# Gate and up columns of a SwiGLU block as one block, with three of its eight k pairs by Strassen's seven products

## The chip, the cores and the metric

The kernel runs on one core of one Trainium2 chip. The metric is the device time of one execution in microseconds (us). The time before is the median of three runs, 1590.43 us (1590.37 to 1591.91).

The engines are named as in the profile: PE (TensorE, matrix products), PEld (its weight loads), DVE (VectorE), ACT (ScalarE), POOL (GpSimd), SP (SyncE, which issues the weight loads from memory here).

## The reference

One layer of a streaming encoder on 256 tokens of width 2048: a norm, an input projection, three token mixers (a recurrence, chunked attention, a state space), gates, an output projection with a residual, and then the part that the change is in:

```python
h = rmsnorm(x, norm_ffn_g[l])
x = x + (jax.nn.silu(h @ w_ffn_gate[l]) * (h @ w_ffn_up[l])) @ w_ffn_down[l]
...
return rmsnorm(x, norm_final_g)
```

`w_ffn_gate` and `w_ffn_up` are 2048 x 5632, `w_ffn_down` is 5632 x 2048, all float32.

## The kernel before

**Precision by three products.** Every weight tile is split into a high part (`hi`, rounded to the type fp32r by an ACT copy) and a low part (`lo`, the exact difference `raw - hi`, a DVE subtraction). Activations are split the same way (`h2h`, `h2l` for the normed input of the feed-forward part). A product is then three matmuls: high x high, low x high, high x low (lines 277 to 279).

**Units and steps.** All weights stream through one list of steps (`steps`, filled by `add_job`, line 225). A step is two k tiles of 128 rows by 512 columns; its body (line 266) issues 2 k tiles x 2 halves of the tokens x 3 = 12 matmuls of 128x512. A job is one block of 512 output columns; its two accumulators (`mm`, one per half of the tokens) lie in two of eight PSUM banks. In PSUM four banks are for `mm`, two for small results (`sm`), and two for the `bu` tile of the state space.

**What sets the order.** The order is written out by hand. The loop at line 1146 does, at step d: issue the load of unit d+5 on SP (four `raw` buffers), copy the high part of unit d+2 on ACT (three `hi` and three `lo` buffers), run what was put off to this step (`later`), issue the matmuls of step d, run what was put off behind them (`later_pe`), and subtract the low part of unit d+2 on DVE. Each engine works through its instructions in that order.

**The feed-forward part.** `ffn_up` (line 998) makes one block n of 512 hidden columns: eight steps of `w_gate`, then eight steps of `w_up`. When the gate sums are done, ACT takes the silu out of PSUM (`sg`); when the up sums are done, DVE multiplies (line 1017); one step later PE turns the product by eight transposes (`at_ps`), and ACT and DVE split it into `at`. Blocks 0 to 5 are part 0 and blocks 6 to 10 part 1; after each part come the columns of `w_down` over the rows of that part. `load_gain` (line 994) loads the gain of the last norm during block 0.

**The rows of `h2`.** In the output projection just before, `turn` (line 976) transposes the residual sum and `parts` (line 980) scales it by the norm's gain and splits it.

Of the kernel before, what the change touches and what calls it, by code (L numbers as in the profile page):

```python
# [27 lines left out]
UK = 2  # L28
RAWB = 4
LEAD = 5  # L30
PARTB = 3
AHEAD = 2
WARM = 9
NORM_STEP = 13
ROOM = 0.4
LO_WEIGHT = 1.22
ROOM_ACT = 1.5
# [23 lines left out]
R_G1, R_G2, R_CW, R_CB, R_BA, R_BX, R_LAM, R_D, R_S5 = 0, 16, 32, 64, 72, 80, 88, 96, 104  # L61
# [58 lines left out]
def trunk(  # L120
# [4 lines left out]
    nc = tc.nc  # L125
# [86 lines left out]
    steps = []  # L212
    raws, his, los = {}, {}, {}
    on_load, on_step, place = {}, {}, {}
    late, late_pe = {}, {}

    def later(n, fn):
# [3 lines left out]
    def later_pe(n, fn):  # L221

        late_pe.setdefault(state["done"] + n, []).append(fn)

    def add_job(src, kt, c0, body, pre=None):

        for k0 in range(0, kt, UK):
            steps.append((src, k0, c0, body, kt, pre if k0 == 0 else None))

    def load_unit(i):  # L230
        if i >= len(steps):
            return
        if i in on_load:
            on_load[i]()
        src, k0, c0 = steps[i][:3]
        raw = wp.tile([P, UK, 512], F32, tag="raw", name="raw", bufs=RAWB)
        raws[i] = raw
        if i > 1:
            nc.sync.dma_start(
                raw, src[k0 * P:(k0 + UK) * P, c0:c0 + 512].rearrange("(k p) n -> p k n", p=P))  # L240
        else:
            for kk in range(UK):
                if i == 0:
                    nc.sync.dma_start(xf[:, kk, :], x_fm[:, kk, :])
                nc.sync.dma_start(raw[:, kk, :], src[(k0 + kk) * P:(k0 + kk + 1) * P, c0:c0 + 512])

    def hi_part(i, kk=slice(None)):
        if i >= len(steps):
            return
        if i not in his:  # L250
            if i in place:
                his[i], los[i] = place[i]()
            else:
                his[i] = wp.tile([P, UK, 512], F32R, tag="hi", name="hi", bufs=PARTB)
                los[i] = wp.tile([P, UK, 512], F32R, tag="lo", name="lo", bufs=PARTB)
        act.copy(his[i][:, kk, :], raws[i][:, kk, :])

    def lo_part(i, kk=slice(None)):
        if i < len(steps):
# [680 lines left out]
    fx = {}  # L940
# [3 lines left out]
    def after_mix():  # L944
# [7 lines left out]
            act.dma_start(fx["x2"], x.rearrange("(h p) d -> p h d", p=P))  # L952
        later_pe(2, residual)

    for n in range(4):
        cs = slice(n * 512, (n + 1) * 512)

        def evac_out(acc, n=n, cs=cs):
            def add():
                x2 = fx["x2"]  # L960
                for h in range(2):
                    vec.scalar_tensor_tensor(x2[:, h, cs], acc[h], 0.5, x2[:, h, cs], ALU.mult, ALU.add)
                later(1, square)
                later_pe(1, turn)

            def square():
                sq = tp.tile([P, 2, 512], F32, tag="t", name="sq")
                for h in range(2):
                    act.activation(sq[:, h, :], fx["x2"][:, h, cs], AF.Square, accum_out=ss4[:, h, n:n + 1])
                if n == 3:  # L970
                    def norm():
                        vec.tensor_reduce(ss, ss4, AX.X, ALU.add)
                        rstd_of(rstd2, ss, scr)
                    later(1, norm)

            def turn():
                for k0 in (4 * n, 4 * n + 2):
                    t = transpose_tokens(lambda h, k: fx["x2"][:, h, k * P:(k + 1) * P], k0, "h2_ps")

# [18 lines left out]
    def ffn_up(part, n, n0):  # L998
        sg = {}

        def evac_gate(acc):
            def do():
                t = fx["fp"].tile([P, 2, 512], F32, tag="sg", name="sg", bufs=2)
                for h in range(2):
                    act.activation(t[:, h, :], acc[h], AF.Silu, scale=rstd2[:, h:h + 1])
                sg[0] = t
            later(1, do)

        def evac_up(acc):
            kb = 4 * (n - n0)  # L1010

            def do():
                if n == n0:
                    at[part] = tuple(fx["fp"].tile([P, 24, S], F32R, tag=f"at{i}", name=f"at{i}") for i in range(2))
                t = sg[0]
                for h in range(2):
                    vec.scalar_tensor_tensor(t[:, h, :], acc[h], rstd2[:, h:h + 1], t[:, h, :], ALU.mult, ALU.mult)
                later_pe(1, turn)

            def turn():  # L1020
                for k0 in (0, 2):
# [5 lines left out]
        add_job(w_gate, KT, n * 512, as_body(lambda: fx["h2"], evac_gate),  # L1027
                (lambda: later_pe(2, load_gain)) if n == 0 else None)
        add_job(w_up, KT, n * 512, as_body(lambda: fx["h2"], evac_up))

    for part, (n0, n1) in enumerate(parts):
        for n in range(n0, n1):
            ffn_up(part, n, n0)
        for c in range(4):
            cs = slice(c * 512, (c + 1) * 512)
            src, kt = w_down[n0 * 512:n1 * 512], 4 * (n1 - n0)
            if part == 1 and c == 3:
                break

            def evac_down(acc, part=part, c=c, cs=cs):  # L1040
                def add():
                    x2 = fx["x2"]
                    for h in range(2):
                        vec.tensor_add(x2[:, h, cs], x2[:, h, cs], acc[h])
                    if part == 1:
                        later(1, square)

                def square():
                    x2 = fx["x2"]
                    sq = tp.tile([P, 2, 512], F32, tag="t", name="sq")  # L1050
                    for h in range(2):
                        act.activation(sq[:, h, :], x2[:, h, cs], AF.Square, accum_out=sq3[:, h, c:c + 1])
                    later(1, scale)

                def scale():
# [175 lines left out]
```

## Time and profile before

| what | value |
|---|---|
| median of three runs | 1590.43 us |
| the profiled execution | 1589.98 us |
| its span, first to last instruction | 1588.2 us |
| PE busy | 1573.7 us (99%), 7193 matmuls and transposes |
| DVE busy | 1028.7 us (65%) |
| ACT busy | 825.1 us (52%) |
| granted clock of PE, mean | 0.998 |

The span is the time between the first and the last instruction of the profiled execution; the rest of its 1589.98 us lies around it. A busy share is a mean over the whole span; the stages differ.

### The profile page before, as it was taken

How to read it: one execution, taken by the hardware profiler on the slowest of the kernel's cores; microseconds unless marked ns; L12 is line 12 of the kernel's file. 1: busy time of each engine (PE TensorE's matmuls, PEld its weight loads, DVE VectorE, ACT ScalarE, POOL GpSimd, SP SyncE). 2: the span in 40 equal slices, each digit the busy share in tenths (PEclk: the TensorE clock that was granted, in tenths of full speed). 3: DMA queues.
4: the chain of work that ended last, by engine and by line, in shares of the span. 5: the costliest groups of instructions: out<-in, count | busy, mean ns of one | idle time of the engine just before them, and what ended most of it. 6: DMA issues, size and time to landing. Idle time of an engine off the chain costs nothing.

```text
span 1588.2 us, 19207 instructions
## 1 busy us (share of the span) xinstructions
PE 1573.7 (99%) x7193; PEld 1296.7 (82%) x7193; DVE 1028.7 (65%) x1183; ACT 825.1 (52%) x1057; POOL 39.8 (3%) x88
## 2 busy tenths in 40 slices
PE   9999999999999999999999999999999999999997
PEld 6888888888888888888888888888888888888885
DVE  5876789988799988566655555454544455545554
ACT  6668675557677645544455444444433444444443
POOL 0011000000000000000000000000000000000000
PEclk9999999999999999999999999999999999999999
DMA  9687757777587766655656665665555666565563
GB/s 326 227 238 222 248 179 211 202 208 192 155 227 196 203 207 186 199 185 187 235 187 212 188 193 184 197 192 186 188 197 192 193 188 192 186 196 190 186 193 127
DMA packets 168558, 317.73 MB, mean 200 GB/s; under 512 B 10625, under 2 KB 23441, under 8 KB 167569
## 3 DMA queue, kind: packets, MB, share of 16 engines
q1 hardware_dynamic: 153632, 296.04, 59.1%
q0 software_dynamic: 11264, 10.49, 3.8%
q10 hardware_dynamic: 3568, 9.98, 1.7%
q8 instruction: 56, 0.92, 0.2%
q14 instruction: 38, 0.30, 0.1%
HBM read 310.17 MB, written 6.30 MB: 199 GB/s over the span
## 4 chain that ended last, share of the span: by engine, by line
PE 97%; DVE 1%; DMA 1%; ACT 0%; issue 0%; SPq 0%; ACTq 0%; DVEq 0%
PE mm L76 93%; PE at_ps L76 1%; PE y_ps L76 1%; PE fm_ps L76 0%; PE bu L76 0%; DVE lo L76 0%; DMA raw<-in_w_in 0%; PE lru_ps L76 0%; PE o_ps L76 0%; PE sc_ps L76 0%; DMA raw<-in_w_ffn_down 0%; DVE res L76 0%; PE h_ps L76 0%; PE mt_ps L76 0%; PE pt_ps L76 0%
## 5 line engine op out<-in xcount | busy, mean ns | idle before, releaser
L76 ACT CAST hi<-raw 128x1024 fp32r<-128x1024 f32 (+1 forms) x546 | 572.5, 1049 | 721.3 <-PE mm L76 677.5
L76 DVE TENSOR_TENSOR lo<-raw,hi 128x1024 fp32r<-128x1024 f32 (+1 forms) x546 | 663.2, 1218 | 432.4 <-ACT hi L76 430.4
L76 PE MATMUL mm<-hi,xth 128*128 128x512 f32 x768 | 303.4, 395 | 1.5 <-ACT hi L76 1.5
L76 PE MATMUL mm<-lo,xth 128*128 128x512 f32 x768 | 299.9, 390 | 0.6 <-DVE lo L76 0.5
L76 PE MATMUL mm<-hi,xtl 128*128 128x512 f32 x768 | 299.2, 390 | 0.0
L76 PE MATMUL mm<-hi,h2h 128*128 128x512 f32 x704 | 274.8, 390 | 0.0
L76 PE MATMUL mm<-lo,h2h 128*128 128x512 f32 x704 | 274.1, 389 | 0.6 <-DVE lo L76 0.6
L76 PE MATMUL mm<-hi,h2l 128*128 128x512 f32 x704 | 273.9, 389 | 0.0
L76 PE MATMUL mm<-hi,at 128*128 128x512 f32 x640 | 197.4, 390 | 0.6 <-ACT hi L76 0.6
L76 PEld LDWEIGHTS mm<-hi,xth 128*128 128x128 f32 x768 | 144.2, 188 | 34.2 <-ACT hi L76 4.6
L76 PEld LDWEIGHTS mm<-lo,xth 128*128 128x128 f32 x768 | 144.2, 188 | 33.2 <-DVE lo L76 2.9
L76 PEld LDWEIGHTS mm<-hi,xtl 128*128 128x128 f32 x768 | 144.3, 188 | 28.6
L76 PEld LDWEIGHTS mm<-lo,h2h 128*128 128x128 f32 x704 | 132.2, 188 | 28.5 <-DVE lo L76 1.1
L76 PEld LDWEIGHTS mm<-hi,h2l 128*128 128x128 f32 x704 | 132.2, 188 | 27.0
L76 PEld LDWEIGHTS mm<-hi,h2h 128*128 128x128 f32 x704 | 132.2, 188 | 27.0
L76 PEld LDWEIGHTS mm<-hi,at 128*128 128x128 f32 x640 | 119.9, 188 | 25.8 <-ACT hi L76 1.1
L76 PE MATMUL mm<-lo,at 128*128 128x512 f32 x320 | 124.6, 389 | 0.5 <-DVE lo L76 0.5
L76 PE MATMUL mm<-hi,yc 128*128 128x512 f32 x256 | 79.1, 390 | 0.0
L76 PEld LDWEIGHTS mm<-lo,at 128*128 128x128 f32 x320 | 60.1, 188 | 13.4 <-DVE lo L76 1.0
L76 PEld LDWEIGHTS mm<-hi,yc 128*128 128x128 f32 x256 | 47.8, 188 | 9.8
L76 PE MATMUL mm<-hi,mth 128*128 128x512 f32 x128 | 50.2, 392 | 0.0
L76 PE MATMUL mm<-lo,mth 128*128 128x512 f32 x128 | 49.8, 389 | 0.0
(181 smaller groups left out, 1297.2 us busy)
## 6 DMA issues: line engine op xcount, KB each, us to landing
raw<-in_w_in SPq DMA_DIRECT2D x190, 512.0 KB, 4.3
raw<-in_w_ffn_gate SPq DMA_DIRECT2D x88, 512.0 KB, 3.5
raw<-in_w_ffn_up SPq DMA_DIRECT2D x88, 512.0 KB, 4.2
raw<-in_w_ffn_down SPq DMA_DIRECT2D x88, 512.0 KB, 4.8
raw<-in_w_branch SPq DMA_DIRECT2D x48, 512.0 KB, 4.7
raw<-in_w_out SPq DMA_DIRECT2D x32, 512.0 KB, 4.6
raw<-in_ssm_w_glu SPq DMA_DIRECT2D x16, 512.0 KB, 4.7
bc<-s_b POOLq DMA_DIRECT2D x24, 128.0 KB, 5.3
```

The costliest lines, as they stand in the source:

```text
L76: return fn(*args, **kw)
```

## The change

Blocks 1 to 10 are made by `ffn_block` in place of `ffn_up`. Block 0 stays as it was.

Gate and up columns of a block run together, with their four sums (two halves of the tokens for gate, two for up) in the four `mm` banks. The sixteen k tiles are eight pairs. Of a pair, the activations form a 2 x 2 matrix of blocks (halves of the tokens by k tiles) and the weights one too (k tiles by gate and up). Three of the eight pairs (`NQ = 3`) are multiplied by the scheme with seven block products instead of eight. It needs sums of the blocks of both matrices:

- of the activations (`left_sums`), made once and split into high and low parts (`lsum`), in the columns n = 0 and n = 1 of the output projection;
- of the weights (`Pair`), made for each pair in each block: `mix` subtracts (1024 wide), `low` makes two more differences (512 wide each) and the low parts; the high parts are ACT copies (`high`). The sums lie in `mix` tiles, their parts in `pmix`.

A pair takes two steps, 9 matmuls in the first and 12 in the second. Three of its products are needed in two or more sums; these lie in the `sm` banks (`p5`, `p1`) and in the `bu` banks (`p67`), and `sum1`, `sum2` and `sum3` add them on DVE after the pairs. `silu` and `product` then add what lies in the `mm` banks. The order of the sixteen steps of a block is `FFN_ORDER`: p0, p1, p2 are the pairs, g and u are steps of gate and up as before. The rows of a pair are loaded by four transfers of 256 KB in place of two of 512 KB, into a tile `praw` with room for two pairs. The transposes of a block's product move into the next block, four of them behind each of two steps. `load_gain` moves to the first columns of `w_down` of part 1.

```diff
+NQ = 3
+FFN_ORDER = 'p0 p0 g p1 p1 u p2 p2 u g g g g u u u'
...
+        if i in paired:
+            return
...
-        act.copy(his[i][:, kk, :], raws[i][:, kk, :])
+        if i in paired:
+            paired[i].high(i)
+        else:
+            act.copy(his[i][:, kk, :], raws[i][:, kk, :])
...
+        if i in paired:
+            paired[i].low(i)
+        elif i < len(steps):
...
+    def left_sums(k0, t):
...
+        if k0 == 0:
+            fx["sum"] = big.tile([P, NQ, 2, 4, P], F32R, tag="B", name="lsum")
+            fx["acc"] = fx["fp"].tile([P, 2, 512], F32, name="acc")
+        w = tp.tile([P, 2, 512], F32, tag="t", name="lw")
+        a = w[:, 0, :].rearrange("p (k s) -> p k s", k=2)
+        sf = w[:, 1, :].rearrange("p (i s) -> p i s", i=4)
+        for i in range(2):
+            act.activation(a[:, i], t[:, i * S:(i + 1) * S], AF.Identity, scale=prm[:, R_G2 + k0 + i:R_G2 + k0 + i + 1])
+        a11, a21, a12, a22 = a[:, 0, :P], a[:, 0, P:], a[:, 1, :P], a[:, 1, P:]
+
+        def sums():
+            act.copy(h2h[:, k0:k0 + 2, :], a)
+            vec.tensor_add(sf[:, 0], a21, a22)
+            vec.tensor_sub(sf[:, 1], sf[:, 0], a11)
+            vec.tensor_sub(sf[:, 2], a11, a21)
+            vec.tensor_sub(sf[:, 3], a12, sf[:, 1])
+
+            def low():
+                act.copy(fx["sum"][:, k0 // 2, 0], sf)
+                vec.tensor_sub(h2l[:, k0:k0 + 2, :], a, h2h[:, k0:k0 + 2, :].bitcast(F32))
+                vec.tensor_sub(fx["sum"][:, k0 // 2, 1], sf, fx["sum"][:, k0 // 2, 0].bitcast(F32))
+            later(1, low)
+        later(1, sums)
+
...
+                        if k0 < 2 * NQ:
+                            left_sums(k0, t)
+                            return
...
+                fx["turn"] = turn
+
+            def turn(k0s=(0, 2)):
+                for k0 in k0s:
...
+    class Pair:
...
+            two = i - self.first
+            for j, src in enumerate((w_gate, w_up) if two == 0 else (w_up, w_gate)):
+                k = 2 * self.q + two
+                nc.sync.dma_start(self.raw[:, 2 * two + j, :], src[k * P:(k + 1) * P, self.n * 512:(self.n + 1) * 512])
+
+        def mix(self, i):
+            if i == self.first:
+                self.t = [tp.tile([P, 2, 512], F32, tag="t", name="mix")]
+                vec.tensor_sub(self.t[0], self.raw[:, 1:3], self.raw[:, 0:2])
+
+        def high(self, i):
+            mixed, raw = fx["mixed"], self.raw
+            if i == self.first:
+                act.copy(mixed[:, 0, 0], self.t[0])
+                act.copy(his[i][:, 0, :], raw[:, 0])
+            else:
+                act.copy(mixed[:, 1, 0], self.t[1])
+                act.copy(his[i], raw[:, 2:4])
+
+        def low(self, i):
+            mixed, raw = fx["mixed"], self.raw
+            if i == self.first:
+                t = tp.tile([P, 2, 512], F32, tag="t", name="mix")
+                self.t.append(t)
+                vec.tensor_sub(t[:, 0], raw[:, 2], self.t[0][:, 0])
+                vec.tensor_sub(t[:, 1], raw[:, 3], t[:, 0])
+                vec.tensor_sub(mixed[:, 0, 1], self.t[0], mixed[:, 0, 0].bitcast(F32))
+                vec.tensor_sub(los[i][:, 0, :], raw[:, 0], his[i][:, 0, :].bitcast(F32))
+            else:
+                vec.tensor_sub(mixed[:, 1, 1], self.t[1], mixed[:, 1, 0].bitcast(F32))
+                vec.tensor_sub(los[i], raw[:, 2:4], his[i].bitcast(F32))
+
+        def body(self, i, k0, kt):
+            b, q = self.block, self.q
+            mixed, lsum = fx["mixed"], fx["sum"]
+            hi, lo = his.pop(i), los.pop(i)
+
+            def x(kk, h):
+                return tuple(t[:, 2 * q + kk, h * P:(h + 1) * P] for t in fx["h2"])
+
+            def s(j):
+                return tuple(lsum[:, q, p, j] for p in range(2))
+
+            def m(t, j):
+                return tuple(mixed[:, t, p, j] for p in range(2))
+
+            if i == self.first:
+                if q == 0:
+                    b["p5"], b["p1"] = sm("p5"), sm("p1")
+                    b["p67"] = ps.tile([P, 2, 512], F32, tag="bu", name="p67", bufs=1)
+                todo = ((b["p5"], s(0), m(0, 0)), (b["p67"][:, 1], s(2), m(0, 1)),
+                        (b["p1"], x(0, 0), (hi[:, 0], lo[:, 0])))
+            else:
+                if q == 0:
+                    b["d"] = [pm.tile([P, 512], F32, tag="mm", name="mm") for _ in range(4)]
+                d = b["d"]
+                todo = ((b["p67"][:, 0], s(1), m(1, 0)), (d[2], x(1, 1), m(1, 1)),
+                        (d[0], x(1, 0), (hi[:, 1], lo[:, 1])), (d[1], s(3), (hi[:, 0], lo[:, 0])))
+            for j, (acc, (xh, xl), (wh, wl)) in enumerate(todo):
+                pe.matmul(acc, xh, wh, start=q == 0, stop=False)
+                pe.matmul(acc, xl, wh, start=False, stop=False)
+                pe.matmul(acc, xh, wl, start=False, stop=q == NQ - 1 and (j == 0 or i == self.first))
...
+        def classic(col, first, final):
...
+                        acc = b["d"][2 * h + col]
+                        hs = slice(h * P, (h + 1) * P)
+                        pe.matmul(acc, xh[:, k, hs], hi[:, kk, :], start=first and col == 1 and h == 1 and kk == 0,
+                                  stop=False)
+                        pe.matmul(acc, xl[:, k, hs], hi[:, kk, :], start=False, stop=False)
+                        pe.matmul(acc, xh[:, k, hs], lo[:, kk, :], start=False,
+                                  stop=final and kk == UK - 1)
+                if final:
+                    later(1, silu if col == 0 else product)
...
+        def silu():
+            t = b["sg"]
+            for h in range(2):
+                vec.tensor_add(t[:, h, :], t[:, h, :], b["d"][2 * h])
+                act.activation(t[:, h, :], t[:, h, :], AF.Silu, scale=rstd2[:, h:h + 1])
+
+        def product():
+            t, u = b["sg"], fx["acc"]
+            for h in range(2):
+                vec.tensor_add(u[:, h, :], u[:, h, :], b["d"][2 * h + 1])
+            for h in range(2):
+                vec.scalar_tensor_tensor(t[:, h, :], u[:, h, :], rstd2[:, h:h + 1], t[:, h, :], ALU.mult, ALU.mult)
+            fx["turn"] = turn
+            if n == n0 + parts[part][1] - parts[part][0] - 1:
+                later_pe(1, fx.pop("turn"))
...
+        def sum1():
+            t, u = fx["fp"].tile([P, 2, 512], F32, tag="sg", name="sg", bufs=2), fx["acc"]
+            b["sg"] = t
+            act.copy(t[:, 0], b["p1"])
+            vec.tensor_add(u[:, 0], t[:, 0], b["p67"][:, 0])
+
+        def sum2():
+            t, u = b["sg"], fx["acc"]
+            vec.tensor_add(t[:, 1], u[:, 0], b["p67"][:, 1])
+            vec.tensor_add(u[:, 0], u[:, 0], b["p5"])
+
+        def sum3():
+            vec.tensor_add(fx["acc"][:, 1], b["sg"][:, 1], b["p5"])
...
+                def pre():
+                    def turns():
+                        t = fx.pop("turn", None)
+                        if t is not None:
+                            t((0,))
+                            later_pe(1, lambda: t((2,)))
+                    later_pe(after + 2, turns)
+                    for m, fn in enumerate((sum1, sum2, sum3)):
+                        later(after + m, fn)
...
-            ffn_up(part, n, n0)
+            if n == 0:
+                ffn_up(part, n, n0)
+            else:
+                ffn_block(part, n, n0)
...
-            add_job(src, kt, c * 512, as_body(lambda part=part: at[part], evac_down))
+            add_job(src, kt, c * 512, as_body(lambda part=part: at[part], evac_down),
+                    (lambda: later_pe(2, load_gain)) if part == 1 and c == 0 else None)
...
+        if d + LEAD + 1 in paired:
+            paired[d + LEAD + 1].load(d + LEAD + 1)
...
+        if d + AHEAD + 1 in paired:
+            paired[d + AHEAD + 1].mix(d + AHEAD + 1)
```

In DVE's order a block boundary looks as follows before: `sg<-mm` is the product of silu and up, `at<-at_ps` the split of the transposes, and each `lo` stands for one step.

```order
L76 TENSOR_TENSOR lo<-raw,hi 128x1024 x14
L76 SCALAR_TENSOR_TENSOR sg<-mm,rstd_108,sg 128x512 x2
L76 TENSOR_TENSOR lo<-raw,hi 128x1024 x2
L76 TENSOR_TENSOR at_7367<-at_ps,at_7366 128x512 x2
L76 TENSOR_TENSOR lo<-raw,hi 128x1024 x14
```

In the changed kernel DVE has the following from the additions of `silu` (`sg<-sg,mm`) to the second pair of the next block, whose first difference is the second `mix<-praw` row.

```order
L78 TENSOR_TENSOR sg<-sg,mm 128x512 x2
L78 TENSOR_TENSOR lo<-raw,hi 128x1024
L78 TENSOR_TENSOR mix<-praw 128x1024
L78 TENSOR_TENSOR mix<-praw,mix 128x512 x2
L78 TENSOR_TENSOR pmix<-mix,pmix 128x1024
L78 TENSOR_TENSOR lo<-praw,hi 128x512
L78 TENSOR_TENSOR pmix<-mix,pmix 128x1024
L78 TENSOR_TENSOR lo<-praw,hi 128x1024
L78 TENSOR_TENSOR acc<-acc,mm 128x512 x2
L78 SCALAR_TENSOR_TENSOR sg<-acc,rstd_108,sg 128x512 x2
L78 TENSOR_TENSOR lo<-raw,hi 128x1024
L78 TENSOR_TENSOR mix<-praw 128x1024
```

So `mix`, its two halves and two `pmix` rows join the `lo` rows, and the four rows of `product` stand between the low parts of pair p0 and the `lo` of the g step behind it.

On PE a step of gate or up before waits for ACT at its first matmul and for DVE at its third, the first that reads `lo`:

```order
L76 MATMUL mm<-hi,h2h 128x512 [waits Activation_49]
L76 MATMUL mm<-hi,h2l 128x512
L76 MATMUL mm<-lo,h2h 128x512 [waits DVE_49]
L76 MATMUL mm<-hi,h2h 128x512
L76 MATMUL mm<-hi,h2l 128x512
L76 MATMUL mm<-lo,h2h 128x512
```

The first step of a pair in the changed kernel, nine matmuls (`p_7745`, `p_7747` and `p_7746` are p5, p67 and p1):

```order
L78 MATMUL p_7745<-pmix,lsum 128x512 [waits PE_49,Activation_49]
L78 MATMUL p_7745<-pmix,lsum 128x512
L78 MATMUL p_7745<-pmix,lsum 128x512 [waits DVE_49]
L78 MATMUL p_7747<-pmix,lsum 128x512 x3
L78 MATMUL p_7746<-hi,h2h 128x512 [waits Activation_49]
L78 MATMUL p_7746<-hi,h2l 128x512
L78 MATMUL p_7746<-lo,h2h 128x512 [waits DVE_49]
```

Its third matmul waits for the low part of the mixed weights (`pmix<-mix,pmix`), which comes behind `mix` and its two halves on DVE.

## Rows read from the trace of the kernel before

**Rows 1.** The page: busy time by engine; the chain that ended last, by engine.

```profile
PE 1573.7 (99%) x7193; PEld 1296.7 (82%) x7193; DVE 1028.7 (65%) x1183; ACT 825.1 (52%) x1057; POOL 39.8 (3%) x88
...
PE 97%; DVE 1%; DMA 1%; ACT 0%; issue 0%; SPq 0%; ACTq 0%; DVEq 0%
```

**Rows 2.** Busy us in stretches: one FFN block, and one stretch of the mixers.

```profile
core 0: us, PE busy (x) PEld busy (x) DVE busy (x) ACT busy (x) POOL busy (x), PEclk, DMA share, GB/s
904.40:948.80 44.40, 44.40 (x202) 36.85 (x201) 22.18 (x20) 18.98 (x21) 0.00 (x0) 1.00 0.62 190
220.00:320.00 100.00, 100.00 (x467) 82.58 (x466) 94.98 (x99) 56.18 (x73) 6.87 (x16) 1.00 0.72 204
```

**Rows 3.** Timeline of PE around one step: start us, us, what.

```profile
1000.45 0.39 PE L76 MATMUL mm<-lo,h2h 128*128 128x512 f32 x1
1000.68 0.39 PE L76 MATMUL mm<-hi,h2h 128*128 128x512 f32 x1
...
1003.40 0.39 PE L76 MATMUL mm<-hi,h2h 128*128 128x512 f32 x1
```

**Rows 4.** Timeline of ACT at the same step; in brackets the idle time before.

```profile
1000.65 1.05 ACT L76 CAST hi<-raw 128x1024 fp32r<-128x1024 f32 x1 [1.67 <-PE mm L76]
```

**Rows 5.** Timeline of DVE at the same step.

```profile
1001.74 1.22 DVE L76 TENSOR_TENSOR lo<-raw,hi 128x1024 fp32r<-128x1024 f32 x1 [1.50 <-ACT hi L76]
```

**Rows 6.** Timeline of DVE where it is never idle (x2: two merged).

```profile
303.01 1.22 DVE L76 TENSOR_TENSOR t<-sn,bu 128x1024 f32<-128x1024 f32 x1
304.14 1.22 DVE L76 TENSOR_TENSOR lo<-raw,hi 128x1024 fp32r<-128x1024 f32 x1
305.28 1.29 DVE L76 TENSOR_TENSOR t<-t,t 128x512 f32<-128x512 f32 x2
...
311.34 1.22 DVE L76 TENSOR_TENSOR t<-cs,t 128x1024 f32<-128x1024 f32 x1
312.60 1.22 DVE L76 TENSOR_TENSOR t<-sn,t 128x1024 f32<-128x1024 f32 x1
...
317.44 0.43 DVE L76 TENSOR_SCALAR cs<-sn 128x512 f32<-128x512 f32 x1
317.90 0.69 DVE L76 SCALAR_TENSOR_TENSOR sn<-cs,sn 128x512 f32<-128x512 f32 x1
...
1024.68 1.43 DVE L76 SCALAR_TENSOR_TENSOR sg<-mm,rstd,sg 128x512 f32<-128x512 f32 x2
```

**Rows 7.** Groups by form: DVE and ACT, busy us and mean ns.

```profile
L76 DVE SCALAR_TENSOR_TENSOR sg<-mm,rstd,sg 128x512 f32<-128x512 f32 x22 | 15.7, 751 | 0.0
L76 DVE TENSOR_TENSOR x<-x,mm 128x512 f32<-128x512 f32 x14 | 9.6, 688 | 3.1 <-PE mm L76 3.1
L76 ACT CAST hi<-raw 128x512 fp32r<-128x512 f32 x4 | 2.5, 615 | 1.0 <-DMA raw<-in_w_in 0.9
L76 ACT CAST at<-at_ps 128x512 fp32r<-128x512 f32 x22 | 11.7, 584 | 0.0
```

**Rows 8.** Timeline of all engines where PE waited for a late `lo`.

```profile
13.05 1.23 DVE L76 TENSOR_TENSOR lo<-raw,hi 128x1024 fp32r<-128x1024 f32 x1 [0.81 <-ACT hi L76]
...
14.34 0.50 PE L76 MATMUL mm<-lo,xth 128*128 128x512 f32 x1 [0.53 <-DVE lo L76]
...
14.68 0.40 PE L76 MATMUL mm<-hi,xth 128*128 128x512 f32 x1
```

**Rows 9.** DMA issues: name, count, KB each, median us from issue to landing.

```profile
raw<-in_w_ffn_gate SPq DMA_DIRECT2D x88, 512.0 KB, 3.5
...
xf<-in_x_fm SPq DMA_DIRECT2D x7, 256.0 KB, 6.4
out<-x SPq DMA_DIRECT2D x6, 256.0 KB, 2.8
```

**Rows 10.** Waits of SP's queue: us in total, times, longest us.

```profile
SPq L239 <- DVE lo L76: 1200.1, 506, 7.6
```

**Rows 11.** The chain that ended last around one block's transposes.

```profile
897.51 0.87 PE at_ps L76 x8
```

More of the change, by code (lines that the diff above doesn't have):

```diff
@@ L214, in trunk @@
     on_load, on_step, place = {}, {}, {}
+    paired = {}
     late, late_pe = {}, {}
@@ L255, in hi_part @@
                 los[i] = wp.tile([P, UK, 512], F32R, tag="lo", name="lo", bufs=PARTB)
-        act.copy(his[i][:, kk, :], raws[i][:, kk, :])
+        if i in paired:
+            paired[i].high(i)
+        else:
+            act.copy(his[i][:, kk, :], raws[i][:, kk, :])
     def lo_part(i, kk=slice(None)):
-        if i < len(steps):
+        if i in paired:
+            paired[i].low(i)
+        elif i < len(steps):
             vec.tensor_sub(los[i][:, kk, :], raws[i][:, kk, :], his[i][:, kk, :].bitcast(F32))
@@ L953, in after_mix @@
         later_pe(2, residual)
+    def left_sums(k0, t):
+        h2h, h2l = fx["h2"]
+        if k0 == 0:
[19 more added lines that the diff above has]
+        later(1, sums)
     for n in range(4):
@@ L1017, in do @@
                     vec.scalar_tensor_tensor(t[:, h, :], acc[h], rstd2[:, h:h + 1], t[:, h, :], ALU.mult, ALU.mult)
-                later_pe(1, turn)
-            def turn():
-                for k0 in (0, 2):
+                fx["turn"] = turn
+            def turn(k0s=(0, 2)):
+                for k0 in k0s:
                     tt = transpose_tokens(lambda h, k: sg[0][:, h, k * P:(k + 1) * P], k0, "at_ps")
@@ L1026, in evac_up, with __init__, load @@
             later(1, do)
-        add_job(w_gate, KT, n * 512, as_body(lambda: fx["h2"], evac_gate),
-                (lambda: later_pe(2, load_gain)) if n == 0 else None)
+        add_job(w_gate, KT, n * 512, as_body(lambda: fx["h2"], evac_gate))
         add_job(w_up, KT, n * 512, as_body(lambda: fx["h2"], evac_up))
+    class Pair:
+        def __init__(self, n, q, block):
+            self.n, self.q, self.block = n, q, block
+        def load(self, i):
+            if "raw" not in fx:
+                fx["raw"] = big.tile([P, 2, 4, 512], F32, tag="TL", name="praw")
+                fx["mixed"] = big.tile([P, 2, 2, 2, 512], F32R, tag="TH", name="pmix")
+            if not hasattr(self, "raw"):
+                self.first = i
+                fx["turns"] = fx.get("turns", 0) + 1
+                self.raw = fx["raw"][:, fx["turns"] % 2]
+            two = i - self.first
[52 more added lines that the diff above has]
+                pe.matmul(acc, xh, wl, start=False, stop=q == NQ - 1 and (j == 0 or i == self.first))
@@ new lines, in ffn_block, with body, turn @@
+    def ffn_block(part, n, n0):
+        b = {}
+        order = FFN_ORDER.split()
+        after = max(i for i, o in enumerate(order) if o[0] == "p") + 1
+        nxt = {"g": 2 * NQ, "u": 2 * NQ}
+        last = {c: max(i for i, o in enumerate(order) if o == c) for c in "gu"}
+        seen = set()
+        def classic(col, first, final):
+            def body(i, k0, kt):
+                xh, xl = fx["h2"]
+                hi, lo = his.pop(i), los.pop(i)
+                raws.pop(i)
+                for kk in range(UK):
+                    k = k0 + kk
+                    for h in range(2):
[8 more added lines that the diff above has]
+                    later(1, silu if col == 0 else product)
+            return body
+        def silu():
[7 more added lines that the diff above has]
+                vec.tensor_add(u[:, h, :], u[:, h, :], b["d"][2 * h + 1])
+            for h in range(2):
+                vec.scalar_tensor_tensor(t[:, h, :], u[:, h, :], rstd2[:, h:h + 1], t[:, h, :], ALU.mult, ALU.mult)
+            fx["turn"] = turn
+            if n == n0 + parts[part][1] - parts[part][0] - 1:
+                later_pe(1, fx.pop("turn"))
+        def turn(k0s=(0, 2)):
+            kb = 4 * (n - n0)
+            if part not in at:
+                at[part] = tuple(fx["fp"].tile([P, 24, S], F32R, tag=f"at{i}", name=f"at{i}") for i in range(2))
+            for k0 in k0s:
+                tt = transpose_tokens(lambda h, k: b["sg"][:, h, k * P:(k + 1) * P], k0, "at_ps")
+                v = tt.rearrange("p (k s) -> p k s", k=2)
+                ks = slice(kb + k0, kb + k0 + 2)
+                later(1, lambda ks=ks, v=v: split(at[part][0][:, ks, :], at[part][1][:, ks, :], v))
+        def sum1():
[9 more added lines that the diff above has]
+            vec.tensor_add(fx["acc"][:, 1], b["sg"][:, 1], b["p5"])
+        for i, o in enumerate(order):
+            pre = None
+            if i == 0:
+                def pre():
[7 more added lines that the diff above has]
+                        later(after + m, fn)
+            if o[0] == "p":
+                if order[:i].count(o) == 0:
+                    pair = Pair(n, int(o[1]), b)
+                paired[len(steps)] = pair
+                steps.append((None, 0, 0, pair.body, KT, pre))
+            else:
+                col = "gu".index(o)
+                k0 = nxt[o]
+                nxt[o] += 2
+                first = o not in seen
+                seen.add(o)
+                steps.append(((w_gate, w_up)[col], k0, n * 512, classic(col, first, i == last[o]), KT, pre))
@@ L1031, in trunk @@
     for part, (n0, n1) in enumerate(parts):
         for n in range(n0, n1):
-            ffn_up(part, n, n0)
+            if n == 0:
+                ffn_up(part, n, n0)
+            else:
+                ffn_block(part, n, n0)
         for c in range(4):
```

## The prediction

> **What bounds the kernel now.** I read the page first: PE is busy for 1573.7 of the 1588.2 us of the span, and the chain that ended last is 97% PE [rows 1]. A busy PE can hide waits, so next the stretch of one feed-forward block: 44.40 us long, PE busy in all of it, granted clock 1.00, DVE busy for 22.18 us, ACT for 18.98 [rows 2]. Then the timeline of one step. Matmuls start 0.23 us apart, and the twelve of a step take 1003.40 - 1000.68 = 2.72 us, 0.2267 each [rows 3]. A block is 192 matmuls and eight transposes: 192 x 0.2267 = 43.53, and 0.87 for the transposes [rows 11], 44.40 together, which is the block's length. There is no gap in it. The feed-forward blocks last as long as their matmuls, and the reader is to see that a matmul less is 0.2267 us less, as long as nothing else comes late.
>
> How much room is there? At a step's start ACT copies the high part for the step two further on (start 1000.65, 1.05 us; it waited for PE to free the buffer [rows 4]), and DVE subtracts the low part from 1001.74 to 1002.96 [rows 5]. It is read by the third matmul of that later step, at 1000.68 + 2 x 2.72 + 0.45 = 1006.57. So DVE is some 3.6 us early, and half idle.
>
> **PE's side of the change.** Per block three pairs lose 3 of 24 matmuls each, 9 of 192; ten blocks, so 90 matmuls x 0.2267 = 20.4 us. The transposes stay eight a block. A changed block without waits is 183 x 0.2267 + 0.87 = 42.36 us.
>
> **DVE's side.** What does an instruction cost when DVE is never idle? In such a stretch (95% busy with PE unharmed [rows 2]) a 1024-wide subtraction lasts 1.22 us but the next begins 1.13 after it (303.01 to 304.14); two of 512 merged take 1.29, so the second begins 0.60 after the first; one that reads what the instruction just before it wrote begins after its end (311.34 to 312.60: 1.26; 317.44 to 317.90: 0.46 for one of 0.43) [rows 6]. I take 1.13 and 0.60, 1.26 and 0.72 where the next one needs the result, and for the 512-wide product with a scale 1.43 - 0.75 = 0.68 [rows 6, 7]. Reading PSUM makes no difference (0.688 against 0.69) [rows 6, 7]. A pair is then 1.26 (mix) + 0.72 + 0.60 (its halves) + 3 x 1.13 + 0.60 (low parts) = 6.57, against 2.26 for two steps before. A block: three pairs 19.7, ten `lo` 11.3, the sums 4 x 0.60, silu's additions 1.2, product 2.56, splits 1.2: 38.4 us of 42.36. DVE goes from half idle to 91% busy, and the load is uneven.
>
> So I add up DVE from the point where it last waits for PE. Let T be the start of step 13, the first of the last three u steps. Silu's first addition may start at T + 0.20 (the matmul before T started 0.23 earlier and lasts 0.39, a signal takes some 0.04, as from ACT's end at 1001.70 to 1001.74 [rows 3 to 5]). Then follow, in DVE's order: additions to 1.40, `lo` of step 15 to 2.53, mix of p0 to 3.79, halves to 5.11, two low parts to 6.84, two more to 9.10, product to 11.66, `lo` of the g step to 12.79 (read at 13.37, in time), mix of p1 to 14.05, halves to 15.37, and the mixed low part ends 1.22 later, at 16.59. PE is at p1's third matmul at 3 x 2.72 + 21 x 0.2267 + 2.72 + 0.45 = 16.09. It waits about 0.55, and a restart cost some 0.1 more (14.34 to 14.68 in place of 0.23) [rows 8]: 0.65. From there to the same matmul of p2, DVE has 0.60 + 2.26 + 1.13 + 1.26 + 1.32 and again 1.22, and ends at 24.29; PE, delayed, is there at 24.22: another 0.2 with the restart. Behind p2 DVE has seven plain steps of 2.72 with 1.13 each and the sums, and catches up. That is 0.85 per block.
>
> In blocks 1 and 6 the step before is plain: no silu additions on DVE, and 1.36 (block 1's plain product) or 1.2 us (the additions behind `w_down`) in place of product's 2.56, so DVE is some 2.4 us earlier and PE does not wait. Eight blocks x 0.85 = 6.8 us.
>
> The page of the Trainium skill "VectorE: DVE Perf Modes", section "The DRAIN you can't avoid", says that after each op the pipeline is emptied and that an op which follows does not start before. By that rule alone a 1024-wide subtraction would cost its full duration each time. The rows above disagree for instructions that do not need each other's result; the same page's section "Two Vector instructions with no wait between them" allows an earlier start for one that is not held. What the first rule would make of the sum is the second rival.
>
> **What is hidden.** ACT: per pair 2 x 1.05 + 0.62 + 1.05 = 3.77 against 2.10, and one copy of 0.58, so about 24.6 of 42.4 us [rows 2, 4, 7]; its copy of `mix` (1.05) runs beside DVE's two halves (1.32). If that cover were gone, the difference is paid once per pair, under 1 us. `left_sums`: three calls of four 128-wide and two 512-wide DVE instructions in place of two scaled splits, a bit over 1 us of DVE each, in steps with 3.6 us of room [rows 5]. Nothing. `load_gain`: one transfer at another place, read ten steps later. Nothing. The transfers: the bytes are the same, but a pair's come in four of 256 KB. A 512 KB load takes 3.5 us; transfers of 256 KB lie between 2.8 and 6.4 [rows 9]. SP stands in wait for free buffers for 1200 us of the span [rows 10], so loads go out as early as buffers allow. The tightest is p0: issued in step 10 or 11, mixed late in step 13, 8 us apart or more. Even 6.4 and four issues fit. From 0 up to 2 us a block if I am wrong; I take 0, since 3.5 is the nearest row.
>
> **Sum.** 1588.2 - 20.4 + 6.8 = 1574.6 for the span, which is 1576.4 for the profiled execution (1589.98 before, 1.8 around the span), and 1576.8 against the median, 0.45 above it. A per cent on DVE's durations moves a block's wait by about 0.25 us (the chain up to p2 is 24 us long), so the forecast's own range is 1572 to 1582.
>
> **Rivals.**
>
> 1. *No waits at all.* DVE is a little faster than I add up (waits end 0.85 us a block, 3.5% of the chain, earlier). For it: the chain is long and its ends are close. Against it: every term is a row. Time 1590.4 - 20.4 = 1570.0.
>
> 2. *DVE cannot overlap its instructions here, and the kernel gets slower.* The place: the same chain, from silu to p2. In the changed kernel nearly every instruction waits for another engine or for the one before. At 1.26, 0.72 and 0.79 apiece the chain reaches the g step's `lo` at 14.34 (1.1 too late with restart), p1's mixed low part at 18.30 (1.25 more) and p2's at 26.76 (1.0 more): 3.35 a block, 26.8 over eight, and 0.3 in each of the other two. Time 1590.4 - 20.4 + 27.4 = 1597. It decides from waits of 2.5 us a block on, a pitch near 1.22, where the overlap is gone. For it: the dependent rows. Against it: `lo` waits for three others before as well, and overlaps in the busy stretch [rows 6].
>
> 3. *Half of it.* The signals between ACT, DVE and PE cost some 0.03 to 0.06 each on this chain, more than in a stretch with room: 1.6 to 2.3 us a block, 1583 to 1588.
>
> 4. *Transfers.* The four of a pair land late at the block's first pair, 2 us in ten blocks: 1590 to 1597. Against it: DMA moves 190 GB/s in a block and 204 in the busier stretch without a wait of PE [rows 2].
>
> That the change does not do what it says is no rival: the changed order has 90 matmuls fewer.
>
> **How the numbers follow.** Forecast 0.63, rival 1 0.09, rival 3 0.12, rival 2 0.10, rival 4 0.06. Less than 0.2% (3.2 us) is about what a measurement cannot tell from no change. Faster by more, below 1587.2: 0.63 + 0.09 + 0.10 of rival 3 = 0.82. Within: 0.02 each of rivals 2, 3 and 4, 0.06. Slower: 0.08 + 0.04 = 0.12. The range leaves out rivals 2 and 4 and little else: 1569 to 1588.
>
> **What would show it.** Right: in a block of about 43.2 us PE has one wait of about half a microsecond at the third matmul of p1 and a smaller one at p2, both for DVE's `pmix`; none at p0; DVE is busy for about 40 us of a block, with pitches of 1.13; blocks 1 and 6 are 42.4 long; ACT and the loads end no wait of PE. Wrong: waits at the g step behind p0 (rival 2), waits of DVE or ACT for `praw` (rival 4), or a block of 42.36 (rival 1).

## The result and the profile after

The changed kernel takes 1576.95 us (median of 4 runs, 1576.4 to 1577.54) against 1590.68 before on the same chip: ratio 0.9912, 95% interval 0.9895 to 0.9929. The forecast was 1576.8, the range 1569 to 1588. The profiled span is 1574.6 us; the sum had 1574.6.

First the page of the changed kernel, to hold against [rows 1]: busy time by engine, the chain that ended last by engine, and two groups of DMA issues (`praw` are those of the pairs; count, KB each, median us to landing).

```profile
PE 1558.5 (99%) x7103; PEld 1277.9 (81%) x7103; DVE 1197.7 (76%) x1425; ACT 871.9 (55%) x1133; POOL 39.9 (3%) x88
...
PE 86%; DVE 9%; issue 2%; DMA 1%; ACT 1%; SPq 0%; ACTq 0%; DVEq 0%
...
raw<-in_w_ffn_gate SPq DMA_DIRECT2D x58, 512.0 KB, 5.4
...
praw<-in_w_ffn_gate SPq DMA_DIRECT2D x60, 256.0 KB, 5.4
```

PE has 7193 - 7103 = 90 matmuls fewer, and the chain, which was 97% PE, now runs through DVE for 9%. Those 9% are not lost time, since PE works beside most of it; they say where to look for the waits, which come to 6.5 us (below).

Next the busy time by stretch, to hold against [rows 2]. The first stretch starts at block 1's second pair, the next is one period of an ordinary block, the last starts at block 6's first pair.

```profile
core 0: us, PE busy (x) PEld busy (x) DVE busy (x) ACT busy (x) POOL busy (x), PEclk, DMA share, GB/s
899.80:942.20 42.40, 42.40 (x193) 35.09 (x192) 37.23 (x42) 21.98 (x27) 0.00 (x0) 1.00 0.60 196
942.45:985.70 43.25, 42.97 (x193) 34.98 (x191) 38.70 (x44) 23.33 (x28) 0.00 (x0) 1.00 0.59 193
...
1239.26:1281.60 42.34, 42.34 (x188) 35.05 (x188) 37.25 (x41) 23.35 (x26) 0.00 (x0) 1.00 0.62 207
```

DVE is busy for 38.7 us of a block instead of 22.18. In the one in the middle PE, which had no gap in [rows 2], is idle for 0.28 us; in the first and the last it has none. The granted clock is 1.00 throughout, so none of this is the clock. PE's waits, over the whole run, have one row for the pairs (us in total, times, longest us):

```profile
PE p L78 <- DVE pmix L78: 1.9, 7, 0.3
```

So no idle time of PE at a pair ends with ACT or with a load. Seven of the eight blocks that wait are in this row; in block 7 the wait at p1, and everywhere the one at p2, is too short to show as idle time.

The timeline of PE at p1 (start us, us, what; in brackets the idle time and what ended it):

```profile
985.34 0.61 PE L78 MATMUL p<-pmix,lsum 128*128 128x512 f32 x2
986.23 1.19 PE L78 MATMUL p<-pmix,lsum 128*128 128x512 f32 x4 [0.28 <-DVE pmix L78]
```

The third matmul starts at 986.23. Without a wait it would have started two pitches behind the first, at 985.34 + 0.45 = 985.79. The wait is thus 0.44 long, although the column of idle time says 0.28: the second matmul (0.39 long from 985.57) still counts as busy while the third is held up. The four matmuls then last 1.19 where 3 x 0.2267 + 0.39 = 1.07 is usual. That makes 0.56 for p1.

The chain of waits of the changed kernel shows the twelve matmuls around the second and third pair as one piece each, `p` x12, and how long the piece took (2.72 is without a wait). Block 1, then an ordinary block:

```profile
899.80 2.72 PE p L78 x12
...
907.28 2.72 PE p L78 x12
...
984.96 1.23 DVE pmix L78
986.23 2.57 PE p L78 x10
...
993.56 2.97 PE p L78 x12
```

p2 waits 2.97 - 2.72 = 0.25; its mixed low part ends on DVE at 993.91, 0.06 after the third matmul was due. Both together are 0.81 per block, and the period of 43.25 is 0.82 above the 42.43 that a block without waits takes (late_product below).

### The profile page after: what moved, and what is told of

Read it like the earlier page. It is cut to its first block, busy times and chain, and to the rows that moved or that the text cites. A ratio compares the mean times of both kernels' runs of the same rounds, so it can differ in the third digit from the quotient of the medians.

```text
span 1574.6 us, 19561 instructions
## 1 busy us (share of the span) xinstructions
PE 1558.5 (99%) x7103; PEld 1277.9 (81%) x7103; DVE 1197.7 (76%) x1425; ACT 871.9 (55%) x1133; POOL 39.9 (3%) x88
## 4 chain that ended last, share of the span: by engine, by line
PE 86%; DVE 9%; issue 2%; DMA 1%; ACT 1%; SPq 0%; ACTq 0%; DVEq 0%
PE mm L78 79%; PE p L78 4%; DVE lo L78 2%; DVE mix L78 2%; DVE pmix L78 2%; DVE sg L78 1%; DVE acc L78 1%; ACT hi L78 1%; PE y_ps L78 1%; PE fm_ps L78 0%; PE bu L78 0%; DMA raw<-in_w_in 0%; PE lru_ps L78 0%; PE at_ps L78 0%; DMA praw<-in_w_ffn_up 0%
## 5 line engine op out<-in xcount | busy, mean ns | idle before, releaser
L78 ACT CAST hi<-raw 128x1024 fp32r<-128x1024 f32 (+1 forms) x486 | 508.2, 1048 | 571.3 <-PE mm L78 514.5
L78 DVE TENSOR_TENSOR lo<-raw,hi 128x1024 fp32r<-128x1024 f32 (+1 forms) x486 | 588.6, 1216 | 226.4 <-ACT hi L78 224.6
L78 PE MATMUL mm<-hi,h2h 128*128 128x512 f32 x494 | 194.0, 393 | 0.0
L78 PE MATMUL mm<-lo,h2h 128*128 128x512 f32 x494 | 192.6, 390 | 0.9 <-DVE lo L78 0.9
L78 PE MATMUL mm<-hi,h2l 128*128 128x512 f32 x494 | 192.3, 389 | 0.0
L78 ACT CAST pmix<-mix 128x1024 fp32r<-128x1024 f32 x60 | 63.0, 1051 | 93.7 <-DVE mix L78 93.5
L78 PEld LDWEIGHTS mm<-lo,h2h 128*128 128x128 f32 x494 | 92.7, 188 | 20.8 <-DVE lo L78 1.4
L78 PEld LDWEIGHTS mm<-hi,h2l 128*128 128x128 f32 x494 | 92.8, 188 | 18.8
L78 PE MATMUL p<-pmix,lsum 128*128 128x512 f32 x270 | 75.2, 396 | 2.0 <-DVE pmix L78 1.9
L78 DVE TENSOR_TENSOR pmix<-mix,pmix 128x1024 fp32r<-128x1024 f32 x60 | 73.1, 1219 | 0.0
```

The lines of the kernel that those rows point to most:

```text
L78: return fn(*args, **kw)
```

## The experiments

Five of the seven kernels change the order of work on DVE or add to it; two change the number of pairs. All are edits of the changed kernel, and their times are medians of 4 runs (8 for more_dve) with 95% intervals of the ratio to the kernel before (1590.5 to 1590.6 us on those chips).

**late_product.** The two scaled multiplications of `product` stand between the low parts of p0 and those of p1. Nothing needs them until the transposes, so they are put off by seven steps:

```diff
-            for h in range(2):
-                vec.scalar_tensor_tensor(t[:, h, :], u[:, h, :], rstd2[:, h:h + 1], t[:, h, :], ALU.mult, ALU.mult)
+            def rest():
+                for h in range(2):
+                    vec.scalar_tensor_tensor(t[:, h, :], u[:, h, :], rstd2[:, h:h + 1], t[:, h, :], ALU.mult, ALU.mult)
...
+                rest()
...
+            else:
+                later(7, rest)
```

> The two scaled multiplications of product (2 x 0.68 us of DVE) are put off by seven steps, out of the chain between silu and the pairs. Theory A (the 0.85 us that a block waits come from the length of DVE's chain from silu to p1 and p2): the chain is 1.36 us shorter than the 0.57 and 0.25 that it is late, both waits of PE go, blocks of 42.36 us, 1576.95 - 6.8 = 1570.1. Theory B (the waits are set by ACT's copy of the mixed weights or by the pairs' transfers, which land after 5.4 us and not after 3.5; DVE is only the last link): 1577, no change.

Measured: 1571.16 us (1570.44 to 1571.4), ratio 0.9878, 0.9861 to 0.9894; span 1568.7. Its chain of waits, one block from p0's last classic matmuls to the next, and the stretch of that block:

```profile
934.64 2.72 PE p L78 x12
...
942.12 2.72 PE p L78 x12
...
962.52 0.44 PE at_ps L78 x4
962.96 2.76 PE mm L78 x12
...
977.07 2.72 PE p L78 x12
```

```profile
934.64:977.07 42.43, 42.43 (x193) 35.17 (x192) 38.70 (x44) 23.43 (x28) 0.00 (x0) 1.00 0.62 199
```

The chain is PE alone, and each piece of a pair is 2.72 long. DVE is busy for the same 38.70 us as in the changed kernel, in a period that is 0.82 us shorter. So DVE's load as such costs nothing; what cost 6 us was the place of 1.3 us of it (two multiplications of 0.66) ahead of p1. With silu_mix_first below, from which its time cannot be told apart, this is the fastest way found, 5.8 us under the changed kernel.

**more_dve.** One more 1024-wide subtraction, whose result nothing reads, ahead of p1's `mix`:

```diff
             if i == self.first:
+                if self.q == 1:
+                    vec.tensor_sub(fx["acc"], self.raw[:, 1:3], self.raw[:, 0:2])
```

> One more 1024-wide DVE subtraction per block, just ahead of the mix of p1, its result unused. Theory A: DVE's chain is 1.13 us longer, all of it is waited for by PE in the eight blocks that wait already, none in blocks 1 and 6: 1576.95 + 9.0 = 1586.0, the first wait of a block near 1.7 us. Theory B: DVE has room, 1577.

Measured: 1586.98 us (1586.14 to 1589.18), ratio 0.9978, 0.9968 to 0.9988; span 1585.0. Two rows of DVE show what the addition costs there, and two of the chain of waits the period:

```profile
984.32 1.22 DVE L78 TENSOR_TENSOR acc<-praw 128x1024 f32<-128x1024 f32 x1
985.46 1.22 DVE L78 TENSOR_TENSOR mix<-praw 128x1024 f32<-128x1024 f32 x1
```

```profile
900.09 3.01 PE p L78 x12
...
944.93 2.58 PE p L78 x10
...
989.31 2.56 PE p L78 x10
```

The `mix` starts 1.14 behind it, and the period is 989.31 - 944.93 = 44.38, 1.13 more: an instruction added ahead of p1 on DVE is paid in full. Eight blocks make 9.0 of the 10.4 us of span. Block 1, which had not waited, now does too (3.01 at 900.09 instead of 2.72), and so does block 6, some 0.5 us each with their p2: theory A missed that. The prediction had DVE 2.4 us earlier there, which less the wait of 0.55 would have left 1.85 of room; what became of it is said further down.

**silu_early.** The order of steps `p0 p0 g p1 p1 u p2 p2 u g g g g u u u` becomes one in which the gate columns end earlier, so that silu's additions leave the place in front of p0:

```diff
-FFN_ORDER = 'p0 p0 g p1 p1 u p2 p2 u g g g g u u u'
+FFN_ORDER = 'p0 p0 g p1 p1 g p2 p2 g g g u u u u u'
```

> The order of steps is p0 p0 g p1 p1 g p2 p2 g g g u u u u u, so that silu's two additions are done two steps ahead of the next block's first mix. Theory A: the chain then begins with the lo of the last step, which waits for ACT's copy (PE's step start + 1.06 + 1.13 = 2.19 in place of 2.53): 0.34 less in each of eight blocks, 1576.95 - 2.7 = 1574.2, though 1.2 us of DVE work leave the chain. Theory B: 1577.

Measured: 1576.09 us (1575.47 to 1577.58), ratio 0.991, 0.9895 to 0.9924; span 1574.5. By the time it cannot be told from theory B's 1577, and by the period neither expectation fits: 1.2 us less on DVE ahead of p0 gave 0.14 a block (986.49 - 943.38 = 43.11), where theory A had 0.34. Its chain of waits points at the loads at one place:

```profile
1010.81 4.64 DMA praw<-in_w_ffn_gate
...
1015.45 1.23 DVE mix L78
```

I took that for the limit at first. But the load issued at 1010.81 is the last of p1's four, and the `mix` at 1015.45 is p0's, whose loads were issued from 1004.92 to 1006.38. DVE's timeline there reads otherwise:

```profile
1014.31 1.23 DVE L78 TENSOR_TENSOR lo<-raw,hi 128x1024 fp32r<-128x1024 f32 x1 [0.88 <-ACT hi L78]
1015.45 1.22 DVE L78 TENSOR_TENSOR mix<-praw 128x1024 f32<-128x1024 f32 x1
```

The `mix` stands 1.14 behind the instruction before it, the ordinary pitch; it is that `lo` that DVE waited 0.88 us for, because ACT had not made the high part. Here is ACT at the same step, in silu_early and then in the changed kernel:

```profile
1013.23 1.05 ACT L78 CAST hi<-raw 128x1024 fp32r<-128x1024 f32 x1 [1.66 <-issue]
```

```profile
1012.93 1.06 ACT L78 CAST hi<-raw 128x1024 fp32r<-128x1024 f32 x1 [1.66 <-PE mm L78]
```

ACT idles 1.66 us in both; the first view names no releaser, the second PE, which frees the buffer. In both the copy starts within 0.03 us of the first matmul of a step on PE (1013.21 and 1012.96). So the high part comes with PE's progress, whatever DVE does before. In the changed kernel it is ready at 1013.99, and the `lo` behind silu's additions starts at 1014.24. So at most 0.25 of the 1.2 us of silu's additions was on the path; the rest lay beside a wait that stays.

The next two kernels test that reading. `mix` needs only the pair's loads, so in both it is moved ahead of that `lo`, for the first pair of a block alone:

```diff
-        lo_part(d + AHEAD)
-        if d + AHEAD + 1 in paired:
-            paired[d + AHEAD + 1].mix(d + AHEAD + 1)
+        nxt = paired.get(d + AHEAD + 1)
+        if nxt is not None and nxt.q == 0:
+            nxt.mix(d + AHEAD + 1)
+        lo_part(d + AHEAD)
+        if nxt is not None and nxt.q > 0:
+            nxt.mix(d + AHEAD + 1)
```

**silu_mix_first**, this edit on top of silu_early.

> silu_early moved silu's two additions on VectorE away from in front of the first pair's steps and gained almost nothing (1576.09 instead of 1576.95). In its trace VectorE then idles 0.88 to 0.89 us per block in front of the low part that stands there (lo at 928.12, 971.24, 1014.31, 1057.38, each <- ACT hi), and the first subtraction of the pair (mix) follows 1.14 behind it. This kernel is silu_early with that mix moved ahead of that low part, for the first pair of a block only. Theory A, the low part waits for ScalarE's high part, which waits for TensorE to free its buffer, so the chain starts no earlier than TensorE's progress lets it: the mix needs neither, fills the idle time, and the rest of the chain comes 1.0 to 1.1 us earlier per block. The wait of 0.68 per block (43.11 - 42.43) is gone: 8 x 0.68 = 5.4 off the span of 1574.5, time 1571. Theory B, the mix waits for the pair's own loads, to which the chain of waits of silu_early is led back at one place (load issued at 1010.81, 4.64 us, mix at 1015.45): the mix starts no earlier, the low part comes 1.1 behind it instead of ahead, and each block grows by up to 1.1: time 1580 to 1585.

Measured: 1570.8 us (1569.62 to 1572.03), ratio 0.9871, 0.9855 to 0.9886; span 1568.8. DVE at the same place, and PE in the chain of waits:

```profile
1011.53 1.22 DVE L78 TENSOR_TENSOR mix<-praw 128x1024 f32<-128x1024 f32 x1
1012.66 1.22 DVE L78 TENSOR_TENSOR lo<-raw,hi 128x1024 fp32r<-128x1024 f32 x1
```

```profile
942.35 2.72 PE p L78 x12
...
984.77 2.72 PE p L78 x12
```

The gap is filled, no `p` piece is longer than 2.72, the period is 984.77 - 942.35 = 42.42. The loads had landed: `mix` could start in the gap. That is theory A, to 0.2 us, and shows that the loads, to which the chain of silu_early was led back, held up nothing.

**mix_first**, the exchange alone, on the changed kernel.

> The changed kernel with the same exchange alone (the first pair's mix ahead of the low part that stands in front of it), silu's additions where they were. There VectorE is busy without a gap from those additions on (969.78, 970.98, 972.11). Theory A: nothing to fill, so the chain starts when it did; only the dependent halves no longer stand right behind their mix (pitch 1.13 instead of 1.26), about 0.1 per block, time 1576. Theory B (the mix waits for its loads): it could not move up, everything behind comes about 1.1 later, 8 blocks, time 1585.

Measured: 1576.25 us (1575.19 to 1577.6), ratio 0.9907, 0.989 to 0.9925; span 1573.4. Its runs overlap with those of the changed kernel, so the period, from p1 to p1 in its chain of waits, has to decide:

```profile
986.12 2.56 PE p L78 x10
...
1029.26 2.56 PE p L78 x10
```

It is 1029.26 - 986.12 = 43.14, 0.11 less than 43.25: about what the dependent halves cost behind their `mix` (1.26 - 1.13). Theory A again. Each edit by itself gives 0.14 or 0.11 a block; the two together take away all 0.82. A gap has to be opened and then filled.

**two_pairs.** Two of eight pairs by the seven products:

```diff
-NQ = 3
-FFN_ORDER = 'p0 p0 g p1 p1 u p2 p2 u g g g g u u u'
+NQ = 2
+FFN_ORDER = 'p0 p0 g p1 p1 u g g g g g u u u u u'
```

> Two pairs of eight by the seven-product scheme instead of three, order p0 p0 g p1 p1 u g g g g g u u u u u. 60 matmuls fewer than before the change, not 90: 13.6 us. Theory A: only p1 waits, and silu lies early as in the run with silu early, so about 0.25 us a block in eight blocks: 1590.7 - 13.6 + 2.0 = 1579.1. Theory B (a cost of 0.23 us with every pair, 6.8 over 30 pairs): 1590.7 - 20 x (0.68 - 0.23) = 1581.7.

Measured: 1580.64 us (1580.37 to 1582.36), ratio 0.9939, 0.9924 to 0.9954; span 1578.7. It lies between the two expectations: the period, from p1 to p1, is 1030.64 - 987.13 = 43.51 in its chain of waits.

```profile
987.13 2.57 PE p L78 x10
1030.64 2.56 PE p L78 x10
```

Without waits it would be 42.43 + 0.68 = 43.11. The 0.4 is a wait at p1, with silu's additions far away, as in silu_early. It looks the same: DVE waits 1.5 us for ACT's high part in front of p0, and the `mix` follows at 1016.53, the ordinary pitch behind.

```profile
1015.38 1.23 DVE L78 TENSOR_TENSOR lo<-raw,hi 128x1024 fp32r<-128x1024 f32 x1 [1.50 <-ACT hi L78]
```

The chain of waits is led back to loads here too, in every block. That ACT and not the loads sets this start was not tested by itself. Two pairs are slower than three with their waits.

**four_pairs.** Four pairs, with the late multiplications of late_product (put off by eight steps):

```diff
-NQ = 3
-FFN_ORDER = 'p0 p0 g p1 p1 u p2 p2 u g g g g u u u'
+NQ = 4
+FFN_ORDER = 'p0 p0 g u p1 p1 g p2 p2 u p3 p3 g g u u'
```

> Four of the eight k pairs by the seven products instead of three, with the late scaled multiplications of late_product. TensorE's own work falls by another 10 x 3 x 0.2267 = 6.8, to a span of 1561.9 if nothing waits. VectorE gets a pair's steps (1.13 + 1.33 + 1.13 + 0.60 + 1.13 + 1.13 = 6.5 at the pitches measured in the changed kernel) and loses two low parts (2.27): 38.4 + 4.2 = 42.6 us of a block in which TensorE has 41.7. Theory A, VectorE becomes the bound of the block: 42.6 if it never idles and up to 43.9 with the idle time it has behind ScalarE and TensorE, so 0.9 to 2.2 of waiting in each of 8 blocks: 1571 to 1582, I take 1580; not better than late_product (1571.2). Theory B, TensorE's matmuls are what counts and VectorE finds its way between them: 1564.

Measured: 1606.0 us (1604.91 to 1607.26), ratio 1.0092, 1.0076 to 1.0108; span 1603.6. Slower than before the change, and both expectations missed. The timeline of PE over one block's start, and DVE at the same place:

```profile
1028.68 0.60 PE L78 MATMUL at_ps<-cst,sg 128*128 128x128 f32 x4
1030.68 1.65 PE L78 MATMUL p<-pmix,lsum 128*128 128x512 f32 x6 [1.41 <-DVE at L78]
1034.75 0.80 PE L78 MATMUL p<-hi,h2h 128*128 128x512 f32 x1 [2.41 <-DVE at L78]
```

```profile
1029.94 0.69 DVE L78 TENSOR_TENSOR at<-at_ps,at 128x512 fp32r<-128x512 f32 x1 [0.81 <-ACT at L78]
...
1034.01 0.68 DVE L78 TENSOR_TENSOR at<-at_ps,at 128x512 fp32r<-128x512 f32 x1
```

The waits end with `at`, not with `pmix`. The transposes and the accumulators p5 and p1 take turns in two PSUM banks (`sm`). With a fourth pair the sums come later, the transposes move behind the last two steps of the block, and the next block's p0 waits for DVE to read their banks; the second read stands 4.07 us behind the first, with a mixed low part, a low part and product's additions between them. And after the longer wait the granted clock falls; this is the same place one period earlier, where that wait ends at 987.08:

```profile
987.08:990.50 3.42, 3.42 (x8) 2.74 (x9) 2.16 (x2) 1.04 (x1) 0.00 (x0) 0.52 0.74 258
```

Eight matmuls in 3.42 us, 0.43 apiece, at a granted clock of 0.52, near the lower of TensorE's two levels (1.2 GHz); before it PE had stood for 1.41 us, worked for 1.66 and stood for 2.40. That is 8 x 0.2 = 1.6 us on top of 3.8 of waiting, most of the 6.0 by which its period (1030.68 - 983.01 = 47.67) exceeds the 41.7 that it would take without waits. So the run does not tell what DVE alone would have cost with four pairs. That stays open: no version with another place for the transposes was run.

## Why the prediction was right, point by point

**PE's side: right, 0.6 us short.** The last transposes of the feed-forward part stand here in the chains of the kernel before, of the changed kernel and of late_product:

```profile
1472.27 0.87 PE at_ps L76 x8
```

```profile
1458.99 0.87 PE at_ps L78 x8
```

```profile
1452.47 0.87 PE at_ps L78 x8
```

Without waits the part ends 19.8 us earlier, not 20.4. The difference is that of the transposes: they now come in two groups of four in nine of the ten blocks, and the step behind each group takes 2.76 instead of 2.72 (late_product's chain). A block without waits is 42.43, not 42.36: 0.07 in nine blocks, 0.6.

**DVE's chain: its length right to a few hundredths, its start named wrongly.** In the changed kernel, from the last wait of DVE ahead of silu's first addition to p1's mixed low part:

```profile
968.04 0.69 DVE L78 TENSOR_TENSOR at<-at_ps,at 128x512 fp32r<-128x512 f32 x1 [1.32 <-ACT at L78]
968.65 1.22 DVE L78 TENSOR_TENSOR lo<-raw,hi 128x1024 fp32r<-128x1024 f32 x1
969.78 1.28 DVE L78 TENSOR_TENSOR sg<-sg,mm 128x512 f32<-128x512 f32 x2
970.98 1.22 DVE L78 TENSOR_TENSOR lo<-raw,hi 128x1024 fp32r<-128x1024 f32 x1
972.11 1.22 DVE L78 TENSOR_TENSOR mix<-praw 128x1024 f32<-128x1024 f32 x1
973.37 1.42 DVE L78 TENSOR_TENSOR mix<-praw,mix 128x512 f32<-128x512 f32 x2
...
984.96 1.22 DVE L78 TENSOR_TENSOR pmix<-mix,pmix 128x1024 fp32r<-128x1024 f32 x1
```

The forecast had 16.59 - 0.20 = 16.39 us from the first addition to the end of the last row; the trace has 986.18 - 969.78 = 16.40. It let the first addition wait for PE, until 0.20 after the start of step 13, which is 969.90 here. In the trace the addition stands at the ordinary pitch behind a `lo`, and DVE's last wait lies one instruction further back, at the transposes' `at`, for ACT. That the addition starts only 0.12 earlier than forecast is luck. DVE is busy for 38.7 us of a block (38.4 in the working). The pitches are the ones taken: 1.13 for independent instructions, 1.26 behind a `mix` that is needed (972.11 to 973.37). That kills rival 2: with no overlap, 3.35 us a block, where 0.82 were measured. The same 0.82 rules out rival 1 (none) and rival 3 (1.6 to 2.3). The Trainium skill's page "VectorE: DVE Perf Modes", section "The DRAIN you can't avoid", lets the next op start only when the pipeline is empty, and adds that one which is not held starts earlier. The rows with a pitch of 1.13 behind instructions of 1.22 go with the addition, for instructions that do not need the one before.

**The waits: right.** 0.56 at p1 (forecast 0.65) and 0.25 at p2 (forecast 0.2), 0.82 per block by the period (forecast 0.85), in eight blocks and none in blocks 1 and 6. Over the part: 1458.99 - 1452.47 = 6.5 us (forecast 6.8). Product's instructions were a term of the chain; late_product took 1.3 us of them away and all waits went.

**Blocks 1 and 6: right that they don't wait, wrong in the room they have.** more_dve shows a wait in block 1 with 1.13 us more, where 1.85 of room follow from the prediction. The changed kernel's DVE in block 1, the `lo` of the last step before p0 and p1's mixed low part, shows why:

```profile
885.06 1.23 DVE L78 TENSOR_TENSOR lo<-raw,hi 128x1024 fp32r<-128x1024 f32 x1 [1.50 <-ACT hi L78]
...
897.84 1.22 DVE L78 TENSOR_TENSOR pmix<-mix,pmix 128x1024 fp32r<-128x1024 f32 x1
```

This `lo` starts 1.06 after the start of step 13 on PE (884.00), the one in an ordinary block 1.28 after it (970.98 and 969.70). So the missing additions of silu bring 0.22, not the 1.2 that the prediction counts: the `lo` waits for ACT's high part instead. Product brings its 1.2. The mixed low part ends at 899.06, and p1's third matmul is at 900.09: 1.0 of room, less than 1.13.

**The transfers: the cover held, the number did not.** I took 3.5 us to landing; the median is 5.4, and the longest of a pair's loads took 7.7. The tolerance had been worked out up to 6.4. Even so, from block 1 to the last block no wait of PE, DVE or ACT ends with a load, which rules out rival 4. silu_mix_first shows that the loads of p0 leave room for a `mix` in the gap ahead of that `lo`.

**ACT, `left_sums`, `load_gain`: nothing, as said.** ACT is busy for 23.3 us of a block (24.6 forecast), and between the last transposes and the end the changed kernel takes 115.61 us against 115.93. So the 13.6 us of span are 20.4 - 0.6 - 6.5 + 0.3, where the forecast had 20.4 - 6.8: the end agrees so closely because what it lacked, 0.6 of loss and 0.3 of gain, and its 0.3 too much of waiting cancel.

**What I got wrong** for blocks 1 and 6, and again in silu_early: I counted the room that an instruction leaves on DVE as time off the chain, without asking when the instruction behind it may start at all. And in four_pairs I priced two engines and forgot the banks.

## What to carry to other kernels

An engine at 91% load is no bound by itself: add up its instructions in their order, from the last point where it waits for another engine (read off a trace, not taken from the plan) to each result that someone reads, at measured pitches. Where a wait shows, look for an instruction ahead of it that nobody needs soon, and put that off; taking one away ahead of a wait that stays gains only the little that the wait leaves. Moving a stage later also moves the release of its PSUM banks: find who gets them next before adding work.

## What was not expected of the hardware

- A wait of PE for a late operand costs more than its idle column shows, 0.44 instead of 0.28, and the matmuls behind it another 0.12 (p1 in the changed kernel; the forecast had 0.1 for this last part).
- Two waits of 1.41 and 2.40 us with 1.66 us of work between them were followed by 3.4 us at a granted clock of 0.52 in four_pairs; single waits of about half a microsecond, in eight of the ten changed blocks of the changed kernel, left it at 1.00.
- Gate loads of 256 KB landed no sooner than those of 512 KB in the changed kernel, 5.4 us each, where the 512 KB ones took 3.5 before [rows 9]; in four_pairs it was 3.1 against 6.4. So the size alone does not set it; what does was not tried.
